# A streaming encoder layer on one core: where background attention runs at the end of two stages, and when the pooling groups are scaled

## The chip, the cores and the metric

The kernel runs on one core of one Trainium2 chip. The metric is the device time of one execution in microseconds (us). A time is the median of several executions, a profile is one execution recorded by the hardware profiler.

## The reference

One layer of a hybrid encoder over 2,080 rows of width 1,024: 2,048 rows of a new stream and 32 rows of a running one, which has 256 cached keys. All in float32.

```python
h = _rmsnorm(x, g_mix)
u = h @ w_in                                   # 1024 -> 512 q, 512 k, 512 v, 512 pooling input
att = _stick_breaking(q, k_all, v_all, ...)    # 8 heads x 64, strictly causal, no softmax:
#   a = sigmoid(z) * prod of sigmoid(-z) over the later keys;  att = a @ v
att = _rmsnorm(att, g_sb_out)
pool = _multiscale_pool(up, ...)               # 4 groups x 128, trailing means over 2/4/8/16 rows minus self,
#   a 128x128 map per group, then _rmsnorm over all four groups with the gain pool_scale
x = x + concat([att, pool]) @ w_out
h2 = _rmsnorm(x, g_ffn)
x = x + (silu(h2 @ w_gate) * (h2 @ w_up)) @ w_down      # D_FF = 2816
gate = sigmoid(_rmsnorm(x, g_ple) @ w_ple_gate)
x = x + (p @ w_ple) * gate
y = _rmsnorm(x, g_final)
```

Keys, values and the last 15 pooling inputs are outputs too.

## The kernel before

**Products.** Activations are kept transposed: features on the 128 partitions, rows along the free axis. Every large product is made exact by splitting both operands into a rounded part and a remainder (`split`: a cast on ScalarE, a subtraction on VectorE, lines 180 and 181), and three matmuls stand for one (`mm3`, lines 215 to 217). Weights go through `wunit`: a 512 KB load on SyncE's queue, a cast on ScalarE (line 199), a subtraction on VectorE (line 200).

**Two chains of stages.** `project` runs three times over pairs of row blocks (`WS`, blocks of 288 or 256 to 384 rows) and makes pooling inputs, values, keys and queries. Then `rest` runs three times over pairs of blocks of 336 or 352 rows (`OS`): output product, feed-forward (gate, up, `down` in groups of four feature tiles), gate of the per-layer embedding (`embed_pair`), final norm. The text calls these three the super-blocks; the third is written in its own way (`tail`).

**Attention as background.** `attention()` is a generator; one `step()` of it issues two score matmuls `z` (line 726; ScalarE turns them into `keep` and `beta`, lines 729 and 730, and so frees the one PSUM bank that `z` has), the scan of `keep` and a product on VectorE (lines 744, 745), the turned weights of an older step (`tp`, line 755, split on ScalarE and VectorE) and the products with the values (`av`, lines 768, 769). `drive` hands out these steps between the pieces of the dense work:

```python
for cost in dense:
    att["credit"] += cost * rate
    while att["gen"] is not None and att["credit"] > 0 and att["next"][0] <= ready:
        att["credit"] -= att["next"][1]
        step()
    if att["credit"] > 0:
        att["credit"] = 0.0
```

`gemm` yields after every two terms (six matmuls) what they cost at 2.4 GHz, `6 * w / 2400.0` for `w` columns: 0.96 for 384, 0.84 for 336, 0.64 for 256. `rate` is 1.1 in the second projection, 1.2 in the third, 0.9 after. A step of a block of three row tiles costs 2 to 3 credits. What is not stepped stays in the generator and comes later; the third super-block starts by stepping all that is left, and the first two step until `NEED` groups are done. The first super-block begins with `yield BUBBLE`, 8 credits at once. Before the change the yields of the last `down` of a super-block count half (`LAST_DOWN`).

TensorE's order is the order in which the program issues its instructions; the other engines' orders come from the framework's planner. Each engine works through its own list in order, and so does each DMA queue.

**Pooling.** `pooled(b, g, ps)` takes the product of group `g` of block `b`, makes the window sums on VectorE and splits the result into a pair of `uu` buffers (three of them). Work that TensorE shall do later is deferred: `defer(n, fn)` runs `fn` after the `n`-th next product (`gemm` ends with `tick()`). `group_map` (the 128x128 map and the squares) runs two products later; after the map of group 3 `pool_norm` makes the sums over the features, `rest` spreads the inverse norm over the partitions (into the single `sq` buffer), and `scaled` multiplies all four groups, splits them and stores them to `HX`, one after another. The products that run meanwhile are those of the values: `v_out` writes `v32` (one of three `u` buffers, which `scaled` takes too), splits it, and sends it out by ScalarE's DMA queue.

Of the kernel before, what the change touches and what calls it, by code (L numbers as in the profile page):

```python
# [12 lines left out]
ALU = mybir.AluOpType  # L13
# [43 lines left out]
PREP_LEAD, PREP_COST = 3, 0.5  # L57
ACT_SLOTS, X_SLOTS = 26, 20
LAST_DOWN = 0.5
RATES = (1.1, 1.2, 0.9, 0.9, 0.9)  # L60


# [17 lines left out]
def stickbreak_step(  # L80
# [8 lines left out]
    V, S, GP, T = nc.vector, nc.scalar, nc.gpsimd, nc.tensor  # L89

    def dma(out, in_, queue=None):
        if out.dtype == F32R:
            out = out.bitcast(F32)
        if in_.dtype == F32R:
            in_ = in_.bitcast(F32)
        (queue or nc.sync).dma_start(out=out, in_=in_)
# [70 lines left out]
    def gcol(key, c):  # L167
        return gt[:, goff[key] + c:goff[key] + c + 1]
# [10 lines left out]
    def split(src, hi, lo):  # L179
        S.copy(hi, src)  # L180
        V.tensor_sub(lo, src, hi.bitcast(F32))  # L181
# [41 lines left out]
    def defer(n, fn):  # L223
        deferred.append([n, fn])
# [126 lines left out]
    def project(sup, pool, st, following):  # L351
# [4 lines left out]
        def tmp(b, tag, bufs=2, dt=F32):  # L356
            return pool.tile([128, WMAX], dt, tag=tag, name=nm(tag), bufs=bufs)[:, :N[b]]

        def pair(b):
            return st["xpool"].tile([128, 2, WMAX], F32R, tag="uu", name=nm("uu"), bufs=3)[:, :, :N[b]]  # L360
# [55 lines left out]
        def pooled(b, g, ps):  # L416

            w = WINS[g]
            up = pool.tile([128, WMAX + 2 * HIST], F32, tag="up", name=nm("up"), bufs=2)[:, :L[b]]
            if b == 0:  # L420
                GP.tensor_copy(up[:, 0:HIST], spT[:, g, :])
                GP.memset(up[:, HIST + DSEQ:HIST + DSEQ + HIST], 0.0)
            else:
                GP.tensor_copy(up[:, 0:HIST], halo[b - 1] [:, g, :])
            for (u0, o0, ln) in segs[b]:
                V.tensor_mul(up[:, u0:u0 + ln], ps[:, o0:o0 + ln], rbc[b][:, o0:o0 + ln])
            GP.tensor_copy(halo[b][:, g, :], up[:, L[b] - HIST:L[b]])
            cur, sh = up, 1
            while sh < w:
                nx = pool.tile([128, WMAX + 2 * HIST], F32, tag="win", name=nm("win"), bufs=2)[:, :L[b]]  # L430
                V.tensor_add(nx[:, 2 * sh - 1:], cur[:, 2 * sh - 1:], cur[:, sh - 1:L[b] - sh])
                cur, sh = nx, 2 * sh
            dd = tmp(b, "u", 3)
            for (u0, o0, ln) in segs[b]:
                V.scalar_tensor_tensor(out=dd[:, o0:o0 + ln], in0=cur[:, u0:u0 + ln], scalar=1.0 / w,
                                       in1=up[:, u0:u0 + ln], op0=ALU.mult, op1=ALU.subtract)
            if b == 0:
                u0 = HIST + DSEQ + HIST
                GP.tensor_mul(dd[:, DSEQ:DSEQ + HIST], cur[:, u0:u0 + HIST], recip[:, g, :])
                GP.tensor_sub(dd[:, DSEQ:DSEQ + HIST], dd[:, DSEQ:DSEQ + HIST], up[:, u0:u0 + HIST])  # L440
            dhl = pair(b)
            dh, dl = dhl[:, 0], dhl[:, 1]
            split(dd, dh, dl)
            if b in hist_of:
                def tail():
                    bank = tp_bank()
                    h0 = hist_of[b][1]
                    T.transpose(bank[:HIST, :128], up[:, h0:h0 + HIST], ident)
                    S.copy(hist[b][:, g * 128:(g + 1) * 128], bank[:HIST, :128])
                    if g == 3:  # L450
                        dma(hist_of[b][0], hist[b])
                defer(1, tail)

            def group_map():
                ps = mm_bank()[:, :N[b]]
                mm3(ps, (wp_hi[:, g, :], wp_lo[:, g, :]), (dh, dl))
                if g == 0:
                    yt[b] = pool.tile([128, 4, WMAX], F32, tag="yt", name=nm("yt"), bufs=2)[:, :, :N[b]]
                S.copy(yt[b][:, g, :], ps)  # L459
                if g == 0:  # L460
                    S.activation(acc[b], yt[b][:, g, :], AF.Square)
                else:
                    sq = tmp(b, "sq", 1)
                    S.activation(sq, yt[b][:, g, :], AF.Square)
                    GP.tensor_add(acc[b], acc[b], sq)
                if g == 3:
                    defer(2, lambda: pool_norm(b))
            defer(2, group_map)

        def pool_norm(b):  # L470
            rp = col_sums([acc[b]], TL[b], SBW)

            def rest():
                rpb = tmp(b, "sq", 1)
                bcast(rp, TL[b], N[b], rpb)


                def scaled():
                    for g in range(4):
                        u = tmp(b, "u", 3)  # L480
                        V.scalar_tensor_tensor(out=u, in0=yt[b][:, g, :], scalar=gcol("pool", g), in1=rpb,
                                               op0=ALU.mult, op1=ALU.mult)
                        uu = pair(b)
                        split(u, uu[:, 0], uu[:, 1])
                        dma(HX[:, 4 + g, :, C0[b]:C0[b] + N[b]].rearrange("a p n -> p a n"), uu)
                defer(1, scaled)
            defer(2, rest)


# [129 lines left out]
        for b in sup:  # L619
            for c in range(2, 4):  # L620
                ps = mm_bank()[:, :N[b]]
                for cost in gemm(ps, proj_terms(ws[c - 2], b)):
                    if b == b1 and nxt and len(nxt["queue"]) > KC:
                        nxt["queue"].popleft()()
                    yield cost
                if b == b0 and nxt:
                    nxt["queue"].popleft()()
                out_qk(b, c, False, ps)
# [247 lines left out]
    def rest(sup, pool, apool):  # L876
# [4 lines left out]
        def tmp(b, tag, bufs=2):  # L881
            return pool.tile([128, OMAX], F32, tag=tag, name=nm(tag), bufs=bufs)[:, :N[b]]
# [190 lines left out]
        def h_terms(w, b):  # L1073
            return [(kpart(w, k), h[b][k]) for k in range(KC)]
# [125 lines left out]
        def down(fs, last):  # L1200
            ng = len(fs)
            oc_n = 8 // ng
            for u in range(KC // oc_n):
                wd = wunit()
                def terms(j, b, f0=0, f1=ng):
                    return [(kpart(wd, i, j * 128, (j + 1) * 128), gvals[fs[i]][b]) for i in range(f0, f1)]

                opened = {}
                if last and tail and u == 0:

                    for j in range(oc_n):
                        for b in sup:
                            ps = opened[j, b] = mm_bank()[:, :N[b]]
                            yield from gemm(ps, terms(j, b, 0, ng // 2), last=False)
                for j in range(oc_n):
                    oc = u * oc_n + j
                    for b in sup:
                        if opened:
                            ps = opened[j, b]
                            yield from gemm(ps, terms(j, b, ng // 2), first=False)  # L1220
                        else:
                            ps = mm_bank()[:, :N[b]]
                            yield from gemm(ps, terms(j, b))
                        V.tensor_add(X[b][oc], X[b][oc], ps)  # L1224
                        if last:
                            ready_h(b, oc, "ple")
# [125 lines left out]
        if not tail:  # L1352
            embed_load(sup[0])

        for cost in down(pend, True):
            yield cost * LAST_DOWN

# [19 lines left out]
        def embed_pair():  # L1379
            for oc in range(KC):  # L1380
                wg, we = wunit(), embed_weight(oc)
                pgs = {}
                for b in sup if oc == 0 else ():

                    pgs[b] = mm_bank()[:, :N[b]]
                    yield from gemm(pgs[b], h_terms(wg, b)[:6], last=False)
                for b in sup:
                    if oc:
                        pgs[b] = mm_bank()[:, :N[b]]
                        yield from gemm(pgs[b], h_terms(wg, b))  # L1390
                    else:
                        yield from gemm(pgs[b], h_terms(wg, b)[6:], first=False)
                    if oc == 0:
                        norm1(b)
                        if b == b1:
                            norm2(b0)
                        embed_in(b)
                        yield 0.8
                for b in sup:
                    yield from gated(b, oc, we, pgs[b])  # L1400
# [153 lines left out]
```

## Time and profile before

| | us |
|---|---|
| median of 3 runs (2855.32 to 2857.84) | 2855.47 |
| the profiled execution, time | 2855.36 |
| its span, first to last instruction | 2853.6 |
| TensorE busy | 2785.0 |
| VectorE busy | 2159.7 |
| ScalarE busy | 1359.5 |

The profiled execution's time is 1.8 us above its span, and 0.1 us from the median. Busy time of TensorE counts a matmul from its start to a modelled end, and successive matmuls overlap, so a busy engine can still run at half clock; the granted clock (PEclk, 1.00 is 2.4 GHz) is read beside it. The projections fill 0 to 557 us, the three super-blocks about 564 to 1,395, 1,395 to 2,205 and 2,205 to the end.

### The profile page before, as it was taken

The numbers are of one execution on the slowest core, as the hardware profiler recorded it, in microseconds if no ns is written. First come the engines' busy times: TensorE is split into PE (matmuls) and PEld (weight loads), VectorE is DVE, ScalarE is ACT, GpSimd is POOL, SyncE is SP. The second block draws the span as 40 slices with busy tenths as digits, with TensorE's granted clock in tenths as the row PEclk, the third lists the DMA queues.
The fourth block names the chain that finished last, engine by engine and source line by source line (L and its number), as shares of the span: only waits on it lengthen the run. The fifth ranks groups of instructions, "written<-read, shape, count | busy, mean of one in ns | idle before, by whom it ended". The sixth has DMA issues, their size and how long they took to land.

```text
span 2853.6 us, 50132 instructions
## 1 busy us (share of the span) xinstructions
PE 2785.0 (98%) x18214; PEld 2740.2 (96%) x18214; DVE 2159.7 (76%) x3681; ACT 1359.5 (48%) x2966; POOL 719.0 (25%) x1222
## 2 busy tenths in 40 slices
PE   8999999899999999999999999999999999999998
PEld 7998889899999999999999999999999999999998
DVE  6476798797878787877888777777764788766677
ACT  5454566564444444455554444444443453333354
POOL 2012233133312222232332212112131343322230
PEclk9999999999999999998999999999999999999999
DMA  6866747783333333323562233333234743222224
GB/s 206 240 197 195 225 153 223 215 243 101 96 116 96 94 96 97 111 86 103 183 195 87 87 108 108 101 105 99 81 100 121 227 125 100 64 78 71 78 82 155
DMA packets 529856, 374.36 MB, mean 131 GB/s; under 512 B 63421, under 2 KB 516861, under 8 KB 529610
## 3 DMA queue, kind: packets, MB, share of 16 engines
q1 hardware_dynamic: 488794, 354.77, 41.6%
q10 hardware_dynamic: 40816, 16.39, 2.1%
q8 instruction: 144, 2.36, 0.4%
q14 instruction: 102, 0.84, 0.1%
HBM read 297.88 MB, written 73.20 MB: 130 GB/s over the span
## 4 chain that ended last, share of the span: by engine, by line
PE 72%; DVE 9%; issue 5%; ACT 3%; DMA 1%; POOL 1%; SPq 0%; ACTq 0%; POOLq 0%; DVEq 0%
PE mm L215 20%; PE mm L216 20%; PE mm L217 19%; PE z L726 4%; PE tp L755 4%; PE av L769 2%; PE av L768 2%; DVE keep L744 2%; DVE wlo L200 1%; DVE wlo L181 1%; DVE beta L745 1%; DVE as L915 1%; DVE aa L181 1%; ACT whi L199 1%; DVE as L181 0%
## 5 line engine op out<-in xcount | busy, mean ns | idle before, releaser
L215 PE MATMUL mm<-as,whi 128*128 128x352 f32 (+1 forms) x3628 | 1202.6, 331 | 5.8 <-DMA as<-hx 3.0
L216 PE MATMUL mm<-as,whi 128*128 128x352 f32 (+1 forms) x3628 | 1166.1, 321 | 0.1
L217 PE MATMUL mm<-as,wlo 128*128 128x352 f32 (+1 forms) x3628 | 1162.0, 320 | 1.2 <-DVE wlo L200 1.1
L215 PEld LDWEIGHTS mm<-as,whi 128*128 128x128 f32 x3628 | 684.2, 189 | 9.5 <-DMA as<-hx 4.0
L217 PEld LDWEIGHTS mm<-as,wlo 128*128 128x128 f32 x3628 | 684.4, 189 | 1.8 <-DVE wlo L200 1.8
L216 PEld LDWEIGHTS mm<-as,whi 128*128 128x128 f32 x3628 | 684.5, 189 | 0.4 <-DVE as L181 0.4
L199 ACT CAST whi<-wraw 128x1024 fp32r<-128x1024 f32 x288 | 302.2, 1049 | 277.2 <-PE mm L216 251.6
L744 DVE TENSOR_TENSOR_SCAN keep<-keep,keep,zeros 128x384 f32<-128x384 f32 (+2 forms) x328 | 320.3, 976 | 106.0 <-ACT keep L729 105.1
L200 DVE TENSOR_TENSOR wlo<-wraw,whi 128x1024 fp32r<-128x1024 f32 x285 | 351.1, 1232 | 57.0 <-ACT whi L199 56.0
L729 ACT ACTIVATE keep<-z 128x384 f32<-128x384 f32 (+3 forms) x464 | 195.5, 421 | 382.6 <-PE z L726 334.3
L741 POOL COPY keep<-keep 128x1 f32<-128x1 f32 (+1 forms) x328 | 147.8, 451 | 485.2 <-DVE keep L744 484.7
L745 DVE TENSOR_TENSOR beta<-beta,keep 128x384 f32<-128x384 f32 (+3 forms) x464 | 235.0, 507 | 32.8 <-POOL beta L734 1.6
L726 PE MATMUL z<-kt,q 128*128 128x384 f32 (+4 forms) x928 | 211.5, 309 | 11.4 <-ACT beta L730 11.3
L181 DVE TENSOR_TENSOR aa<-tp,aa 128x384 fp32r<-128x384 f32 (+4 forms) x472 | 212.8, 451 | 12.7 <-ACT aa L180 11.8
L180 ACT CAST aa<-tp 128x384 fp32r<-128x384 f32 (+4 forms) x472 | 192.8, 408 | 54.4 <-PE tp L755 48.3
L1224 DVE TENSOR_TENSOR xs<-xs,mm 128x352 f32<-128x352 f32 (+1 forms) x288 | 143.6, 509 | 87.6 <-PE mm L217 86.6
L755 PE MATMUL tp<-ident,beta 128*128 128x128 f32 (+1 forms) x1112 | 199.4, 273 | 2.3 <-DVE xt L344 1.5
L215 PE MATMUL mm<-hh,whi 128*128 128x384 f32 (+2 forms) x576 | 198.2, 344 | 2.8 <-ACT yt L459 1.6
L730 ACT ACTIVATE beta<-z 128x384 f32<-128x384 f32 (+3 forms) x464 | 194.4, 419 | 7.0 <-ACT keep L729 5.0
L908 POOL TENSOR_TENSOR acc<-acc,sq 128x352 f32<-128x352 f32 (+1 forms) x111 | 120.6, 1087 | 290.5 <-ACT sq L907 290.5
L216 PE MATMUL mm<-hl,whi 128*128 128x384 f32 (+2 forms) x576 | 185.8, 323 | 1.0 <-DVE hl L338 1.0
L217 PE MATMUL mm<-hh,wlo 128*128 128x384 f32 (+2 forms) x576 | 185.6, 322 | 0.4 <-DVE wlo L200 0.4
(206 smaller groups left out, 4408.5 us busy)
## 6 DMA issues: line engine op xcount, KB each, us to landing
wraw<-in_w_ffn_down_dram SPq DMA_DIRECT2D x66, 512.0 KB, 3.5
wraw<-in_w_ffn_gate_dram SPq DMA_DIRECT2D x58, 512.0 KB, 4.0
wraw<-in_w_ffn_up_dram SPq DMA_DIRECT2D x58, 512.0 KB, 3.9
wraw<-in_w_in_dram SPq DMA_DIRECT2D x48, 512.0 KB, 4.8
wraw<-in_w_out_dram SPq DMA_DIRECT2D x48, 512.0 KB, 5.0
kt<-ks SPq DMA_DIRECT2D x112, 192.0 KB, 2.4
vt<-vs SPq DMA_DIRECT2D x112, 192.0 KB, 2.6
wraw<-in_w_ple_gate_dram SPq DMA_DIRECT2D x32, 512.0 KB, 3.8
```

The lines of the kernel that those rows point to most:

```text
L181: V.tensor_sub(lo, src, hi.bitcast(F32))
L199: S.copy(hi, raw)
L200: eng.tensor_sub(lo, raw, hi.bitcast(F32))
L215: T.matmul(ps, a[0], b[0], start=first, stop=False)
L216: T.matmul(ps, a[0], b[1], start=False, stop=False)
L217: T.matmul(ps, a[1], b[0], start=False, stop=last)
L726: T.matmul(z[:qw, :wi], hd["q"][:, e, qsl], un["k"][:, :wi], start=(e == 0), stop=(e == 1))
L729: S.activation(keep[:qw, :wi], z[:qw, :wi], AF.Sigmoid, scale=-0.125)
L730: S.activation(beta[:qw, :wi], z[:qw, :wi], AF.Sigmoid, scale=0.125)
L744: V.tensor_tensor_scan(rev, rev, zeros[:qw].broadcast_to([qw, wi]), initial=init, op0=ALU.mult, op1=ALU.add)
L745: V.tensor_mul(beta[:qw, :wi], beta[:qw, :wi], keep[:qw, 1:wi + 1])
L755: T.transpose(bank[:kw, qo[i]:qo[i] + qws[i]], un["b"][i][:qws[i], k0:k0 + kw], ident[:qws[i], :qws[i]])
```

## The change

Four edits. (1) The yields of a super-block's last `down` count half up to the twentieth, and nothing from there to the thirty-second, so `drive` issues no step of attention there. (2) The first pieces of `embed_pair` (six terms for each of the two blocks, oc 0) yield 0 instead of their cost. (3) In the third projection the last four query products (c 2 and 3 of both blocks) yield 0.4 of their cost. (4) In the pooling norm the map of group 3 runs one product later, `scaled` treats one group per product instead of four at once, and the first block of a pair gets a buffer of its own (`rpb`) for the spread inverse norm.

```diff
+LAST_QUERIES = 0.4
-            defer(2, group_map)
+            defer(3 if g == 3 else 2, group_map)
         def pool_norm(b):
             rp = col_sums([acc[b]], TL[b], SBW)
             def rest():
-                rpb = tmp(b, "sq", 1)
+                rpb = tmp(b, "rpb" if b == b0 else "sq", 1)
                 bcast(rp, TL[b], N[b], rpb)
-                def scaled():
-                    for g in range(4):
-                        u = tmp(b, "u", 3)
...
-                defer(1, scaled)
+                def scaled(g):
+                    u = tmp(b, "u", 3)
+                    V.scalar_tensor_tensor(out=u, in0=yt[b][:, g, :], scalar=gcol("pool", g), in1=rpb,
+                                           op0=ALU.mult, op1=ALU.mult)
+                    uu = pair(b)
+                    split(u, uu[:, 0], uu[:, 1])
+                    dma(HX[:, 4 + g, :, C0[b]:C0[b] + N[b]].rearrange("a p n -> p a n"), uu)
+                    if g < 3:
+                        defer(1, lambda: scaled(g + 1))
+                defer(1, lambda: scaled(0))
             defer(2, rest)
...
-                    yield cost
+                    yield cost * LAST_QUERIES if last else cost
...
-        for cost in down(pend, True):
-            yield cost * LAST_DOWN
+        for i, cost in enumerate(down(pend, True)):
+            yield cost * LAST_DOWN if i < 20 else 0.0
...
-                    yield from gemm(pgs[b], h_terms(wg, b)[:6], last=False)
+                    for _ in gemm(pgs[b], h_terms(wg, b)[:6], last=False):
+                        yield 0.0
```

## Rows read from the trace of the kernel before

**Rows 1.** The page: engine totals, and the chain that ended last, by engine.

```profile
PE 2785.0 (98%) x18214; PEld 2740.2 (96%) x18214; DVE 2159.7 (76%) x3681; ACT 1359.5 (48%) x2966; POOL 719.0 (25%) x1222
...
PE 72%; DVE 9%; issue 5%; ACT 3%; DMA 1%; POOL 1%; SPq 0%; ACTq 0%; POOLq 0%; DVEq 0%
```

**Rows 2.** What TensorE waited for, whole span: total us, times, longest.

```profile
PE z L726 <- ACT beta L730: 11.3, 11, 3.1
...
PE mm L215 <- DMA as<-hx: 3.0, 3, 1.3
```

**Rows 3.** Stretches: length, busy (count) PE PEld DVE ACT POOL; PEclk, DMA share, GB/s.

```profile
65.00:75.00 10.00, 7.81 (x51) 6.93 (x50) 4.56 (x12) 4.04 (x11) 2.40 (x4) 0.83 0.54 148
...
245.00:260.00 15.00, 13.68 (x100) 13.11 (x99) 10.81 (x26) 8.37 (x25) 0.85 (x4) 0.89 0.90 304
...
555.00:575.00 20.00, 14.56 (x76) 12.42 (x75) 11.93 (x24) 8.25 (x21) 1.58 (x8) 0.83 0.92 312
...
1281.28:1305.88 24.60, 21.46 (x103) 19.19 (x101) 16.36 (x31) 12.35 (x28) 7.54 (x11) 0.67 0.34 100
...
2066.00:2100.00 34.00, 34.00 (x216) 34.00 (x216) 17.92 (x32) 11.02 (x19) 6.19 (x6) 1.00 0.38 117
...
2129.21:2140.74 11.53, 11.09 (x79) 10.67 (x79) 7.52 (x15) 5.94 (x13) 4.93 (x7) 1.00 0.31 91
```

**Rows 4.** TensorE in time, around the end of the first super-block's last down.

```profile
1274.59 0.42 PE L215 MATMUL mm<-as,whi 128*128 128x336 f32 x1 [0.73 <-DVE xs L1224]
...
1275.62 0.51 PE L726 MATMUL z<-kt,q 128*128 128x384 f32 x2
...
1276.57 0.40 PE L215 MATMUL mm<-as,whi 128*128 128x336 f32 x1
...
1287.26 0.31 PE L217 MATMUL mm<-as,wlo 128*128 128x336 f32 x1
...
1290.72 1.01 PE L726 MATMUL z<-kt,q 128*128 128x384 f32 x2 [3.14 <-ACT beta L730]
...
1305.88 0.63 PE L215 MATMUL mm<-as,we 128*128 128x336 f32 x1
```

**Rows 5.** VectorE in time: end of the projections, ends of both last downs.

```profile
561.17 0.41 DVE L181 TENSOR_TENSOR aa<-u,aa 128x256 fp32r<-128x256 f32 x1
...
1266.59 2.71 DVE L915 SCALAR_TENSOR_TENSOR as<-xs,gt,as 128x336 fp32r<-128x336 f32 x1
...
2115.98 2.33 DVE L915 SCALAR_TENSOR_TENSOR as<-xs,gt,as 128x352 fp32r<-128x352 f32 x1 [0.80 <-ACT as L914]
```

**Rows 6.** GpSimd in time, the same moment.

```profile
1266.20 2.73 POOL L200 TENSOR_TENSOR wlo<-wraw,whi 128x1024 fp32r<-128x1024 f32 x1
```

**Rows 7.** TensorE in time: its waits in the three projections.

```profile
67.52 0.58 PE L215 MATMUL mm<-uu,wp_hi 128*128 128x384 f32 x1 [1.82 <-ACT uu L180]
...
95.06 0.39 PE L215 MATMUL mm<-whi,hh 128*128 128x256 f32 x1 [0.88 <-ACT v L546]
...
250.68 0.28 PE L768 MATMUL av<-aa,vt 32*128 32x32 f32 x1 [1.32 <-DVE attT L667]
...
433.48 0.38 PE L215 MATMUL mm<-uu,wp_hi 128*128 128x256 f32 x1 [0.85 <-ACT uu L180]
...
464.46 0.44 PE L726 MATMUL z<-kt,q 128*128 128x128 f32 x2 [1.35 <-ACT beta L730]
```

**Rows 8.** TensorE in time, from the projections to the first output product.

```profile
556.57 0.28 PE L217 MATMUL mm<-hh,wlo 128*128 128x256 f32 x1
...
564.45 0.42 PE L215 MATMUL mm<-as,whi 128*128 128x336 f32 x1 [1.28 <-DMA as<-hx]
```

**Rows 9.** The DMA queue of SyncE in time, the same stretch.

```profile
562.03 10.95 SPq L96 DMA_DIRECT2D as<-hx  x15
```

**Rows 10.** TensorE's score matmuls z: count, ns min/median/max, first and last start.

```profile
L726 PE MATMUL z<-kt,q x928: 178/334/689, 168.5 to 2051.0; 128*128 128x384 f32 x96, 128*128 128x256 f32 x67, 128*128 128x128 f32 x16, 128*32 128x32 f32 x4
```

**Rows 11.** DMA issues of the value stores: count, KB each, median us to landing.

```profile
out_dram<-v ACTq DMA_DIRECT2D x32, 128.0 KB, 3.5
```

More of the change, by code (lines that the diff above doesn't have):

```diff
@@ L473, in rest @@
             def rest():
-                rpb = tmp(b, "sq", 1)
+                rpb = tmp(b, "rpb" if b == b0 else "sq", 1)
                 bcast(rp, TL[b], N[b], rpb)
-                def scaled():
-                    for g in range(4):
-                        u = tmp(b, "u", 3)
[L481 to L485, printed above, removed]
-                defer(1, scaled)
+                def scaled(g):
[8 more added lines that the diff above has]
+                defer(1, lambda: scaled(0))
             defer(2, rest)
```

## The prediction

> **What bounds the kernel now.** I read the engine totals first: TensorE is busy 98% of the span and the chain that ended last runs through it for 72% [rows 1]. So only time in which TensorE stands still, or runs at half clock, can be won; work that is merely moved costs TensorE the same wherever it goes. Then the list of what TensorE waited for: the dearest single kind is `z` waiting for `beta`, 11.3 us in 11 waits [rows 2], that is, attention standing in TensorE's own order before ScalarE and VectorE are through with older work. Then the timeline of TensorE for the places. The longest of these waits, 3.14 us, lies at 1,287 to 1,290 us, just behind the last `down` of the first super-block [rows 4]. Smaller ones lie in the projections [rows 7] and where the output product begins [rows 8]. Last the stretches with their clock: around the long wait the mean granted clock is 0.67, so most of that stretch ran at 1.2 GHz [rows 3].
>
> **Edits 1 and 2, the end of the last down.** The yields cut: 12 of 0.84 at half weight and 6 of 0.84 at full weight, times the rate 0.9, are 4.5 + 4.5 = 9.1 credits, about three steps at up to 3 credits. The trace has three in that place: the `z` at 1,275.62, one in the first piece of `embed_pair`, and the one at 1,290.72 that waits [rows 4]. They are postponed, not saved: one step takes TensorE 0.95 us (1,275.62 to 1,276.57).
>
> What the stall costs is read against the second super-block, where attention is over: its last `z` starts at 2,051.0 [rows 10]. From the first matmul of `embed_pair` to the first of the embedding product the first super-block takes 24.60 us, the second 11.53 us at clock 1.00 for the same products [rows 3]; blocks of 352 instead of 336 columns make the second a little longer, one row piece fewer a little shorter, and I let these cancel. Of the 13.07 us of difference some 2.4 us are three attention steps (one of them short), which remain work. That leaves 10.7 us: the 3.14 us wait, the half clock after it, and smaller waits for the norms. I take off 0.9 us, since a wait like that of 0.73 us for a PSUM bank at 1,274.59 [rows 4] can come once more: VectorE is late before the twentieth yield already. **Gain 9.8 us**; the bounds are 10.7 and 0 (the wait reappears whole at the next product that needs `as` or a norm). In the second super-block the edits find nothing to cut as long as attention ends before its last `down`. All three edits postpone 18 credits, six or seven steps. All attention costs 1,152 credits (8 heads times 8 for the running stream and 3 + 12 + 21 + 30 + 39 + 31 for the blocks) and runs for 1,882 us [rows 10], 0.61 per us, so it ends some 30 us later, at about 2,081. The last `down` there (192 matmuls at 34.00/216 us each [rows 3], 30 us before 2,129.21) starts at about 2,099. The forced steps of the third super-block, which would cost most, are 100 us further off.
>
> **Edit 4, the map of group 3.** TensorE waits 1.82 us for the split of the pooled rows in the first projection and 0.85 us in the third [rows 7]. One value product more in front is 24 x 256 / 2,400 = 2.56 us of matmuls at full clock, more than either wait. Around the first wait the clock of 10 us averages 0.83 [rows 3], which is 1.7 us. Sum 4.4 us; I take **4.0**, with 0 as the lower bound if the value product put in front waits for ScalarE, which is in order behind the same split.
>
> **Edit 4, one group per product.** In the burst four groups of each block stand in VectorE's and ScalarE's lists, and three waits of TensorE lie in these bursts: 0.88, 1.32 and 1.35 us [rows 7]; around the second the clock is 0.89 over 15 us [rows 3], 1.65 us more. Sum 5.2 us. Spread out, the same VectorE work remains and the three `uu` and three `u` buffers stay shared, so I take half, **2.6 us**, bounds 5.2 and a loss (the rival below). The own buffer for block `b0` keeps the spread norm alive over four products without holding up `sq`. It also moves tiles in memory, so some load of the output product can wait for another tile. The nearest row is the 3.0 us that TensorE waits for such loads [rows 2]; as much again is the bound, and I take nothing. `HX` is read much later, and SyncE's queue gets its stores in eight portions over five products instead of eight at once, so the loads of keys and values behind them wait less, not more.
>
> **Edit 3, the last queries.** 8 x 0.96 + 8 x 0.64 = 12.8, times 1.2 = 15.4 credits become 6.1: three to four steps leave the stretch before 556.57. Then VectorE splits the last query at once instead of at 561.17 [rows 5], and SyncE's queue can issue the loads of the output product, 15 of them from 562.03 on [rows 9], one to three us sooner relative to the last projection. But TensorE gets there sooner too, with only the steps of `BUBBLE` to fill the time until the loads land: 7.6 us lie between the last query's matmul and the first output product [rows 8]. TensorE's idle time of 5.4 us in that stretch (20.00 minus 14.56) and its clock of 0.83 [rows 3] therefore mostly stay. **Gain 1.5 us**, bounds 3.4 (the clock's part, 20 x 0.17) and minus 3.0 (the wait for the loads [rows 2] once more).
>
> **Postponed steps.** Six or seven steps land between other products than now, and all later ones shift with them. A `z` waits 11.3 us / 464 steps = 0.02 us on average [rows 2, 10], but one unlucky meeting costs up to 3.14 us and clock. I take **minus 1.0**, bounds plus 2 and minus 6.
>
> **Sum.** 9.8 + 4.0 + 2.6 + 1.5 - 1.0 = 16.9 us off the profiled execution's 2,855.36, which stands 0.1 us from the median: 2,838.5 us. What a measurement of this kernel can tell from no change is 0.2%, 5.7 us.
>
> **A rule against it.** At 1,266.59 VectorE's `as` (line 915) takes 2.71 us, while GpSimd subtracts a gate weight from 1,266.20 on for 2.73 us; in the second super-block it takes 2.33 us, with no attention there [rows 5, 6]. The Trainium skill (SBUF — State Buffer, section Who interferes with whom) says that a VectorE instruction with two SBUF inputs contends with a GpSimd instruction that reads SBUF, and that the second to come is blocked for the whole of the other. This row agrees. By that rule the lateness of VectorE is in part no matter of attention, and this change leaves it in.
>
> **The rivals.**
> First: VectorE's lateness comes from that GpSimd subtraction. All 2.7 us of it then show up as TensorE waiting at the last two terms of the gate, and the clock falls as now, which with the small waits is what remains of 10.7 after 3.14, 7.5 us. Edits 1 and 2 give 10.7 - 2.7 - 7.5 = 0.5 us, the sum is 7.6, the time 2,847.8. For it: the row itself. Against it: the second super-block has the same block and TensorE's clock stays at 1.00 [rows 3]. Chance 0.17.
> Second, the change does not do what it says: the waits only move, to the norm behind the last down and to the next value products, and what is won in one place is lost with the postponed steps. Time 2,853, within 0.2%. For it: VectorE is busy 76% of the span, and 16.36 of the 24.60 us even where TensorE stands [rows 1, 3], so it is a second bound close by. Against it: the longest waits name attention's own results, not those of the products. Chance 0.13.
> Third, slower: one group per product sets `v32` against two `u` of `scaled` in three buffers. Then each value product's `v32` must wait until its predecessor has been sent out, and ScalarE, in order, holds `keep` and `beta` behind it. The 0.88 us for `v` [rows 7] is such a wait. A store takes 3.5 us from issue to landing [rows 11], a value product 2.56 us by its cost: 0.9 us each, doubled where the DMA engines are at 0.90 of their time [rows 3]. Three products in each of three projections at 1.9 us are 17 us, and with edit 4's gains gone (6.6) the time is 2,838.5 + 17 + 6.6 = 2,862. It decides from the point at which the wait exceeds what the PSUM banks in hand cover. Against it: two products' worth of banks are in hand. Chance 0.08.
> The forecast keeps 0.62.
>
> **Numbers.** The forecast's own range is 2,831 (bounds of edits 3 and 4 met: 5 to 8 us more) to 2,846; the first rival lies in 2,843 to 2,852, the second in 2,850 to 2,857. From 2,831 to 2,853 holds eight in ten: above lie the third rival and half of the second, below a few in a hundred. Faster by over 0.2%, below 2,849.8: 0.62 and 0.13 of the first rival, 0.75; within 0.2%: the rest of the first, most of the second and a little of the third, 0.18; slower 0.07.
>
> **What would show it.** Right: no `z` between the twentieth yield and the embedding product, that stretch at 12 to 14 us with clock 1.00, no wait of the map for `uu`, attention ending near 2,081. Wrong: a wait of over 2 us at the last two terms or at the sums of the norm, PEclk 0.5 there; ScalarE waiting for `v` stores in every value product; the first output product still over 7 us behind the last query with longer waits for `as`.

## Result and the profile after

The changed kernel takes 2841.7 us, the median of 6 runs (2838.47 to 2843.89), against 2857.56 for the kernel before beside it (6 runs). The ratio is 0.9944, 95% interval 0.9934 to 0.9955: 16.0 us are won, where 16.9 were forecast. The predicted 2838.5 lies 3.2 us below the measured time, and the time lies inside the range. A second comparison of the same two programs (E12 below) gave 0.9944 again.

The profiled execution took 2842.7 us, its span is 2840.3, so the profiles differ by only 12.7 us. First the engine totals of its page, and the chain that ended last by engine:

```profile
PE 2776.3 (98%) x18214; PEld 2734.5 (96%) x18214; DVE 2152.5 (76%) x3681; ACT 1361.0 (48%) x2966; POOL 711.4 (25%) x1222
...
PE 82%; DVE 8%; issue 3%; ACT 3%; DMA 2%; POOL 1%; ACTq 0%; SPq 0%; POOLq 0%; DVEq 0%
```

The instructions are the same in number as in [rows 1]. What fell is time in which TensorE stood or ran slowly: more of the chain is now TensorE itself. Its waits over the whole span (total us, times, longest):

```profile
PE z L728 <- ACT beta L732: 6.5, 7, 1.8
...
PE mm L216 <- DMA as<-hx: 5.1, 1, 5.1
```

Lines of the changed kernel stand one to three higher than before. The waits of `z` fell from 11.3 to 6.5 us, and the longest of 3.1 us is gone [rows 2]. The loads of the output product went the other way: one wait of 5.1 us stands where three made 3.0.

TensorE in time, first at the entry to the first super-block, from the last query product to the first output product, and then behind that super-block's last `down`, from the first product of the embedding gate to the first embedding product (the number in brackets is the wait before the instruction):

```profile
543.47 0.28 PE L218 MATMUL mm<-hh,wlo 128*128 128x256 f32 x1
543.58 0.52 PE L728 MATMUL z<-kt,q 128*128 128x384 f32 x2
...
545.84 0.62 PE L728 MATMUL z<-kt,q 128*128 128x384 f32 x2 [1.06 <-ACT beta L732]
...
547.48 0.62 PE L728 MATMUL z<-kt,q 128*128 128x384 f32 x2 [0.67 <-ACT beta L732]
...
553.86 0.65 PE L216 MATMUL mm<-as,whi 128*128 128x336 f32 x1 [5.08 <-DMA as<-hx]
...
1265.19 0.40 PE L216 MATMUL mm<-as,whi 128*128 128x336 f32 x1 [0.25 <-DVE xs L1226]
...
1274.19 0.51 PE L728 MATMUL z<-kt,q 128*128 128x256 f32 x2
...
1277.11 1.36 PE L278 MATMUL tp<-ident,r 32*128 32x32 f32 x8 [0.32 <-DVE ss L264]
...
1279.30 0.42 PE L728 MATMUL z<-kt,q 128*128 128x128 f32 x2
...
1280.70 0.63 PE L216 MATMUL mm<-as,we 128*128 128x336 f32 x1
```

And stretches, with the granted clock in the third column from the end (length, busy time and count of each engine, PEclk, DMA share, GB/s):

```profile
60.00:80.00 20.00, 19.75 (x163) 19.00 (x161) 11.40 (x22) 10.97 (x27) 5.98 (x7) 1.00 0.65 173
...
546.00:572.00 26.00, 20.25 (x116) 18.97 (x117) 15.02 (x24) 9.99 (x22) 4.07 (x8) 0.87 0.92 315
...
1265.19:1280.70 15.51, 15.10 (x99) 13.70 (x99) 11.20 (x23) 9.93 (x23) 6.15 (x11) 0.97 0.53 155
1280.70:1285.29 4.59, 4.59 (x26) 4.59 (x25) 3.12 (x8) 1.74 (x6) 0.42 (x3) 0.74 0.69 206
...
2269.40:2282.00 12.60, 12.60 (x63) 12.60 (x64) 5.84 (x15) 5.07 (x13) 0.96 (x2) 0.73 0.48 156
```

From the gate's first product to the embedding product there are 15.51 us with two attention steps in them, where there were 24.60 with three at a clock of 0.67 [rows 3, 4]. The first projection runs at 1.00 past the place of the 1.82 us wait [rows 7]. The entry is worse than before: 10.39 us lie between the last query's matmul and the first output product (553.86 minus 543.47), against 7.88 [rows 8]. The last row is one place that can account for the profiles differing by less than the medians. It follows a wait of 2.14 us in the third super-block. The profiled execution of the kernel before had the same wait there and kept its clock:

```profile
2287.28 0.75 PE L256 MATMUL tp<-ones,acc 128*128 128x1 f32 x6 [2.12 <-DVE acc L908]
...
2287.28:2300.00 12.72, 12.72 (x83) 12.72 (x84) 8.72 (x21) 6.58 (x16) 0.96 (x2) 1.00 0.59 198
```

12.60 us at 0.73 are 3.4 us; with them the profiles would differ by 16.1 us, as the medians do. None of the four edits touches that place.

### The profile page after: what moved, and what is told of

It reads as the page before. It is cut to its first block, busy times and chain, and to the rows that moved or that the text cites. A ratio compares the mean times of both kernels' runs of the same rounds, so it can differ in the third digit from the quotient of the medians.

```text
span 2840.3 us, 50159 instructions
## 1 busy us (share of the span) xinstructions
PE 2776.3 (98%) x18214; PEld 2734.5 (96%) x18214; DVE 2152.5 (76%) x3681; ACT 1361.0 (48%) x2966; POOL 711.4 (25%) x1222
## 4 chain that ended last, share of the span: by engine, by line
PE 82%; DVE 8%; issue 3%; ACT 3%; DMA 2%; POOL 1%; ACTq 0%; SPq 0%; POOLq 0%; DVEq 0%
PE mm L216 23%; PE mm L217 22%; PE mm L218 22%; PE z L728 4%; PE tp L757 4%; PE av L770 2%; PE av L771 2%; DVE wlo L201 1%; DVE keep L746 1%; ACT whi L200 1%; DVE win L432 1%; DVE beta L747 1%; PE tp L278 1%; PE tp L257 1%; DVE as L917 0%
```

## The experiments

Theory: edits 1 and 2 take away a meeting of attention with a late VectorE (the wait of `z` and the half clock behind it), the later map takes away the waits for `uu`, the spread smooths VectorE's work, and edit 3 brings little, because the loads set the entry. Rivals: VectorE is late because of GpSimd's subtraction beside it; the waits only move; the spread costs waits for buffers. In all, 12 kernels ran, each beside the kernel before on its chip (its medians 2857.9, 2856.15 and 2856.47 in the three jobs). Gains in us are one minus the ratio, times that median.

**E1, edits 1 and 2 alone.**

```diff
-        for cost in down(pend, True):
-            yield cost * LAST_DOWN
+        for i, cost in enumerate(down(pend, True)):
+            yield cost * LAST_DOWN if i < 20 else 0.0
...
-                    yield from gemm(pgs[b], h_terms(wg, b)[:6], last=False)
+                    for _ in gemm(pgs[b], h_terms(wg, b)[:6], last=False):
+                        yield 0.0
```

> Edits 1 and 2 alone (no attention in the last 12 yields of the last down, none in the first pieces of the gate). Theory: the stall behind the last down was attention waiting for attention, and it goes. The stretch from the first gate product to the first embedding product falls from 24.6 us to 13 to 16 us, its clock rises from 0.67 to above 0.9, and the whole kernel gains 8 to 10 us (ratio about 0.9967). Rival (VectorE is late because of GpSimd's subtraction, or the wait moves to the norm): a wait of 2 us or more in the same place, gain under 2 us.

Measured: 2845.44 us, ratio 0.9957 [0.9943, 0.9972], 12.3 us won (8.0 to 16.3). TensorE in time, and the stretch from the gate to the embedding product:

```profile
1273.43 0.42 PE L215 MATMUL mm<-as,whi 128*128 128x336 f32 x1 [0.74 <-DVE xs L1224]
...
1279.89 0.39 PE L215 MATMUL mm<-as,whi 128*128 128x336 f32 x1 [0.63 <-DVE xs L1224]
...
1292.69 0.59 PE L726 MATMUL z<-kt,q 128*128 128x384 f32 x2
...
1279.89:1293.72 13.83, 13.74 (x91) 12.47 (x92) 9.55 (x20) 8.41 (x18) 6.39 (x9) 1.00 0.38 115
```

The only `z` of the stretch comes 1.03 us before the embedding product, the clock is 1.00, and 13.83 us stand in place of 24.60. Two waits for VectorE's sums of the `down` (`xs`, which frees a PSUM bank), 0.74 and 0.63 us, stay. The mean granted clock of every run is on record too: on average 0.9909 in the 23 runs of the kernel before and 0.9948 in E1's six. The 0.0039 between them are 11 us of the span, an estimate that takes TensorE as the pace all along: nearly all that E1 won is TensorE's clock.

**E6, edit 1 alone** (the first half of the diff above).

> Edit 1 alone: no credit from the twentieth yield of a super-block's last down on, embed_pair's first pieces yielding their cost as before. Edits 1 and 2 together took 12.5 us. Theory that the credit is the cause, wherever it is handed out: 4.5 of 9.1 credits are cut, the step in the first piece of embed_pair and the waiting z behind it stay, gain 3 to 5 us, ratio 0.998 to 0.999, and the z after the down still waits over 1 us for beta. Theory that VectorE's lateness at the end of the down is built up by the steps inside the down: with these gone the z in embed_pair finds its bank free, no wait over 1 us there, gain 9 us or more, ratio 0.997 or less.

Measured: 2853.16 us, ratio 0.9991 [0.9982, 0.9999], 2.6 us won (0.3 to 5.1). TensorE in time, and the stretch from the gate to the embedding product:

```profile
1284.75 0.51 PE L726 MATMUL z<-kt,q 128*128 128x384 f32 x2
...
1291.58 1.54 PE L1093 MATMUL tp<-ident,pn 32*128 32x32 f32 x8 [1.99 <-DVE aa L181]
...
1280.97:1300.12 19.15, 17.16 (x96) 15.68 (x96) 12.68 (x24) 10.33 (x22) 6.86 (x11) 0.83 0.32 97
```

The step inside `embed_pair` no longer waits, as the second theory had it, but it does not win the 9 us that theory named. Its work stands on VectorE ahead of the norm's, and TensorE's next turn (`pn`, the rows of the per-layer input) waits 1.99 us for the last of it, the split `aa`. VectorE in time:

```profile
1288.65 1.01 DVE L744 TENSOR_TENSOR_SCAN keep<-keep,keep,zeros 128x384 f32<-128x384 f32 x1
1289.79 0.56 DVE L745 TENSOR_TENSOR beta<-beta,keep 128x384 f32<-128x384 f32 x1
...
1290.96 0.56 DVE L181 TENSOR_TENSOR aa<-tp,aa 128x384 fp32r<-128x384 f32 x1
1291.44 0.27 DVE L263 TENSOR_SCALAR ss<-tp 32x1 f32<-32x1 f32 x3
```

The clock falls behind this wait too, though for a shorter time: the stretch takes 19.15 us at 0.83, where it was 24.60 at 0.67 and, with both edits, 13.83 at 1.00.

**E7, edit 2 alone** (the second half of the diff).

> Edit 2 alone: embed_pair's first pieces hand out no credit, the yields of the last down all count half as before. Edits 1 and 2 together stood at 0.9957, edit 1 alone at 0.9991 (its profile had no wait of z at the end of the down, but a wait of 1.99 us of the final norm's turn for VectorE's split, and the half clock as before). Theory that one step is one too many wherever it stands, and that both edits are needed: TensorE still waits over 1 us between the down and the embedding product and the clock falls there, ratio 0.998 to 1.000. Rival, that the step inside embed_pair is what does the harm: no wait over 1 us and clock 1.00 there, ratio 0.995 to 0.997, all of what the two edits win.

Measured: 2856.81 us, ratio 0.9999 [0.9991, 1.0008]: nothing. TensorE in time, and the same stretch:

```profile
1276.40 0.51 PE L726 MATMUL z<-kt,q 128*128 128x384 f32 x2
...
1292.60 0.77 PE L1093 MATMUL tp<-ident,pn 32*128 32x32 f32 x4 [1.27 <-DVE ss L263]
...
1282.06:1300.34 18.28, 16.63 (x91) 14.66 (x89) 13.08 (x24) 10.09 (x22) 6.42 (x10) 0.82 0.33 99
```

Here the late steps of the `down` are the ones left, and now the same turn waits for the norm's sums (`ss`, line 263) and the clock falls. This profile's stretch is 6.3 us shorter than that of the kernel before, and yet the medians show nothing won; where E7 loses it again stays open. 2.6 and 0.3 us alone, 12.3 together: in both profiles the steps that remain leave a wait of over 1 us with a fallen clock behind it.

**E8, the changed kernel without GpSimd's subtraction.** The first column of the gate's weights is split by VectorE.

```diff
-            plan_col(w_pgate, (i % KC) * 128, V if i else GP)
+            plan_col(w_pgate, (i % KC) * 128, V)
```

> The changed kernel with the first column of the embedding gate's weights split by VectorE instead of GpSimd, so that no GpSimd subtraction stands beside VectorE's product for the second block at the end of the last down. Forecast: that blocked 2.3 us instruction holds up nothing in the changed kernel (TensorE did not wait for it), so the time stays at 0.994 to 0.995 of the kernel before, and VectorE's product takes under 1 us. First rival (the GpSimd subtraction is what makes VectorE late): another 2 to 5 us are won, ratio 0.9925 to 0.9937, with the stretch from the last down to the embedding product down from 15.5 us. Third possibility: the subtraction itself, now 1 to 2 us of VectorE's own time, makes the norm late, ratio above 0.9955.

Measured: 2841.01 us, ratio 0.9952 [0.9939, 0.9965], the changed kernel's time within the intervals. VectorE (DVE) and GpSimd (POOL) in time, first in the changed kernel, then in this one:

```profile
1251.55 2.39 POOL L201 TENSOR_TENSOR wlo<-wraw,whi 128x1024 fp32r<-128x1024 f32 x1
1251.98 2.33 DVE L917 SCALAR_TENSOR_TENSOR as<-xs,gt,as 128x336 fp32r<-128x336 f32 x1 [0.81 <-ACT as L916]
```

```profile
1250.25 1.24 DVE L201 TENSOR_TENSOR wlo<-wraw,whi 128x1024 fp32r<-128x1024 f32 x1 [0.33 <-ACT whi L200]
1251.14 1.11 POOL L910 TENSOR_TENSOR acc<-acc,sq 128x336 f32<-128x336 f32 x1 [0.73 <-ACT sq L909]
1251.41 1.22 DVE L917 SCALAR_TENSOR_TENSOR as<-xs,gt,as 128x336 fp32r<-128x336 f32 x1
```

The blocked product of 2.33 us becomes 1.22, not under 1 us as expected: GpSimd's sum of squares now runs beside it, and products of this form that begin while GpSimd is idle take 0.57 us in both profiles. VectorE does the subtraction itself in 1.24, and the time stays: the 0.9925 to 0.9937 that the first rival asked for lies outside the interval. VectorE's lateness from this subtraction is real and decides nothing here.

**E3, edit 4 whole, E4, the later map alone, and E5, the spread alone.**

```diff
-            defer(2, group_map)
+            defer(3 if g == 3 else 2, group_map)
```

E4 is this line; E5 is the rest of edit 4 (`rpb`, and `scaled` for one group at a time); E3 is both.

> Edit 4 alone (map of group 3 one product later, one group per product, own buffer). Theory: 6 to 9 us gained, nearly all of it in the first projection and some in the third (ratio about 0.9975). Rival: the spread groups make ScalarE wait for the value stores at every product and half of the gain is lost, 3 us or less.

> Only the later map of group 3; the four groups still in one burst, no buffer of its own. Theory: the waits of 1.82 us and 0.85 us for the split go, and with the clock 4 us are gained (0.9986); the wait of 0.88 us for the value evacuation stays. Rival: the wait only moves to the value product put in front, gain under 1 us.

> Edit 4 without the later map: one group per product and the own buffer rpb, group 3's map after two products as before. Forecast as it was predicted: the bursts are gone, 2.6 us less than the kernel before, ratio about 0.999. Rival, suggested by the later map alone at 0.9978 against 0.9969 for all of edit 4: the spread moves the same work and gains under 1 us; the first z then starts near 168.5 us as before, and the wait of the map for uu in the first projection stays at about 1.8 us, ratio 0.999 to 1.001. Third rival of the prediction: value products wait for buffers, ratio above 1.002 and ScalarE waiting for stores of v.

Measured: E3 2849.16 us, ratio 0.9969 [0.9957, 0.998], 8.9 us won; E4 2851.23, 0.9978 [0.9967, 0.9989], 6.3 us (3.1 to 9.4); E5 2852.18, 0.9988 [0.9979, 0.9996], 3.4 us (1.1 to 6.0). What the matmuls of the map waited for, in E5, over the span (us, times):

```profile
  ACT uu L180: 2.7, 2
  DVE uu L181: 0.5, 1
```

In all eight profiles with the later map this list is empty. The first `z` of attention tells what the first projection gained. In the six profiles without the later map it starts between 166.3 and 168.5 us, in the eight with it between 161.9 and 164.0 (161.9 and 164.0 are one program, the changed kernel, twice); the means, 167.3 and 163.1, are 4.1 us apart. The spread takes away TensorE's wait of 0.88 us for `v` in the first projection [rows 7] and brings it none for a buffer; what VectorE waits for is told with the third rival below.

**E9, the changed kernel without the spread.**

```diff
-                rpb = tmp(b, "rpb" if b == b0 else "sq", 1)
+                rpb = tmp(b, "sq", 1)
...
-                def scaled(g):
...
-                    if g < 3:
-                        defer(1, lambda: scaled(g + 1))
-                defer(1, lambda: scaled(0))
+                def scaled():
+                    for g in range(4):
...
+                defer(1, scaled)
```

> All of the change but the spread: edits 1 to 3 and group 3's map one product later, the four groups scaled in one burst, one buffer for the spread inverse norm. If the spread is worth what was predicted (2.6 us), this kernel stands at 0.9953 of the one before, 0.0009 above the changed kernel's 0.9944. If the spread is worth nothing, it stands at 0.994 to 0.995, and the last turn of the first projection, the first z (near 162 us) and the last z come out as in the changed kernel within 2 us. If the burst is the better form, it is below 0.993.

Measured: 2842.93 us, ratio 0.9953 [0.9941, 0.9965]. E9 against the changed kernel, E4 against E3 and E5 by itself put the spread at 0.0009, 0.0009 and 0.0012, about 2.5 to 3.4 us; only E5's interval leaves out a gain of zero.

**E2, edit 3 alone.**

```diff
+LAST_QUERIES = 0.4
...
-                    yield cost
+                    yield cost * LAST_QUERIES if last else cost
```

> Edit 3 alone (the last four query products hand out 0.4 of their credits). Theory: the output product starts some 10 us earlier less the three to four postponed steps, so 1 to 2 us are gained, and one long wait for the loads of 4 to 5 us takes the place of several short ones (ratio 0.9993 to 1.0). Rival: VectorE is freed for the whole start of the first super-block too, gain 4 us or more (0.9985). Second rival: nothing is gained since TensorE has less to do until the loads land, or up to 3 us are lost.

Measured: 2852.62 us, ratio 0.9982 [0.9973, 0.9991], 5.1 us won (2.6 to 7.7). TensorE in time:

```profile
555.48 0.28 PE L218 MATMUL mm<-hh,wlo 128*128 128x256 f32 x1
...
565.28 0.65 PE L216 MATMUL mm<-as,whi 128*128 128x336 f32 x1 [4.50 <-DMA as<-hx]
...
1286.97 1.01 PE L727 MATMUL z<-kt,q 128*128 128x384 f32 x2 [4.28 <-ACT beta L731]
```

The last query is earlier (555.48 against 556.57) and the first output product later (565.28 against 564.45 [rows 8]). The postponed steps come back behind the last `down`, where `z` now waits 4.28 us. By the same measure the 5.1 us of the medians are TensorE's clock: it averages 0.9939 in E2's twelve runs, against 0.9909 before, which by the estimate of E1 is 8.6 us, more than was won. In this profile one such place is the stretch from the gate to the embedding product, 1278.34 to 1302.15 us, with a clock of 0.86 in spite of the longer wait. Why the clock holds better there is not shown.

**E11, edits 1 and 2 with the later map alone** (neither edit 3 nor the spread).

> Edits 1 and 2 with the later map, and neither edit 3 nor the spread. If the parts add up, 0.9957 and 0.9978 give 0.9935, and with edit 3 left out the first output product starts near 576 us as with the later map alone. If the whole wins less than its parts because edits 3 and 1 spend the same room (postponed steps come back elsewhere), this kernel is as fast as the changed one, 0.994 to 0.995. If edit 3 is worth its 0.0018 in company too, it stands at 0.9955 to 0.9965.

Measured: 2838.26 us, ratio 0.9938 [0.9926, 0.995], 17.7 us won. E1 and E4 add up to 0.9935, so these parts add. TensorE's waits from 540 to 582 us:

```profile
PE mm L215 <- DMA as<-hx: 2.7, 3, 1.4
PE z L726 <- ACT beta L730: 1.6, 2, 1.2
PE av L769 <- DVE aa L181: 0.8, 2, 0.6
```

5.1 us of waits, close to the 5.4 of the kernel before, and not the single long one of the changed kernel. E9 is this kernel plus edit 3, and stands 0.0015 above it, where edit 3 alone stood 0.0018 below the kernel before. The two intervals of E9 and E11 overlap, so it isn't shown that edit 3 costs time in company; that it is not worth its 5.1 us there is (minus 4.3, give or take 4.9, from the intervals' half widths of 3.4 us each). The mean clock of the runs says the same, 0.9948 in E9 and 0.9964 in E11: 4.5 us.

**E10, the changed kernel with more attention at the entry.**

```diff
-BUBBLE = 8.0
+BUBBLE = 16.0
```

> The changed kernel with BUBBLE at 16 credits instead of 8, so two to four more steps of attention stand between the last query and the first output product, where TensorE of the changed kernel waits 5.08 us in one piece for as<-hx. Theory that the loads set that moment and that the steps fit into the time: the first output product starts at the same distance from the last query's product, the wait is under 2 us, and 2 to 4 us are won against the changed kernel, ratio 0.9930 to 0.9937. Rival, that attention is itself bound there by VectorE's scans: TensorE waits for beta instead of for as, the first output product comes as late or later, ratio 0.994 to 0.996.

Measured: 2837.97 us, ratio 0.993 [0.9917, 0.9942], 20.0 us won, the lowest of all. TensorE in time, and a stretch of 26 us, to be held against that of the changed kernel above:

```profile
546.11 0.28 PE L218 MATMUL mm<-hh,wlo 128*128 128x256 f32 x1
546.22 0.52 PE L728 MATMUL z<-kt,q 128*128 128x384 f32 x2
...
555.20 0.48 PE L728 MATMUL z<-kt,q 128*128 128x256 f32 x2
...
557.01 0.63 PE L216 MATMUL mm<-as,whi 128*128 128x336 f32 x1
...
549.00:575.00 26.00, 23.24 (x138) 21.31 (x137) 20.28 (x37) 13.44 (x32) 7.74 (x17) 0.93 0.95 320
```

The first output product follows the last query by 10.90 us, hardly later than the 10.39 of the changed kernel. Six steps of attention lie in that time instead of three, the wait for `as` is gone, `z` waits 2.9 us there instead of 1.7, and the clock of the stretch is 0.93 instead of 0.87. The first load has landed at 555.9 us, so the steps run 1.1 us past the moment that the loads set.

**E12, the changed kernel again**, on the chip of E7, E10 and E11.

> The changed kernel itself, on the same chip as the three others: the measure for what they win or lose against it. By the first comparison 0.9944 [0.9934, 0.9955]. The sum of the parts measured alone (0.9957, 0.9982, 0.9969) is 0.9908. If the parts add up, it comes out at or below 0.993; if the whole is less than its parts, at 0.994 to 0.9955.

Measured: 2841.61 us, ratio 0.9944 [0.9932, 0.9956]. E10 is 3.6 us below it by the medians and E11 3.4; their intervals overlap with its own, so that either beats the changed kernel is likely and not settled.

## Why the prediction came out

**The forecast's way and its sum hold; the terms in it are off and cancel.** The edits alone win 12.3 (edits 1 and 2), 8.9 (edit 4) and 5.1 us (edit 3), 26.3 together, where 17.9 were forecast; the whole wins 16.0. The gains were put 8.4 us too low, and what the edits take from one another 9.3 us too low. That the sum came within 0.9 us is therefore luck, while the main stall and its price were read rightly.

**Edits 1 and 2**, forecast 9.8, bounds 0 and 10.7: 12.3, interval 8.0 to 16.3. The reading against the second super-block named the right stretch and about its price: 13.83 us at 1.00 in E1, where 12 to 14 were said. The price was read from one profile, and the clock does not fall each time. E5 keeps the three steps and a wait of 3.15 us, and loses far less behind it than the kernel before:

```profile
1280.62:1300.55 19.93, 16.70 (x102) 14.98 (x101) 15.97 (x30) 11.96 (x27) 6.88 (x11) 0.91 0.32 92
```

The same stretch takes 24.02 us at 0.71 in E3 and 24.60 at 0.67 in E4. So how much of the price one execution pays varies, and it is the mean clock of E1's runs that carries the reading. In the changed kernel itself two steps come between the turns of the norm, the stretch takes 15.51, and a wait of 0.32 us is followed by a clock of 0.74 for 4.6 us; behind the same wait in E9 the clock is 1.00. The statement that no `z` stands between the twentieth yield and the embedding product was wrong: only the yields of `embed_pair`'s first six terms count nothing, and credit flows again from the terms and norms behind them. What the prediction did not see is that neither edit is worth much without the other (E6, E7).

**The first rival** (GpSimd's subtraction) falls with E1 and E8. E1 keeps the block whole and wins 12.3 us all the same:

```profile
1265.43 2.70 DVE L915 SCALAR_TENSOR_TENSOR as<-xs,gt,as 128x336 fp32r<-128x336 f32 x1
```

In E8 the block is shortened and the time is the same. The Trainium skill (SBUF — State Buffer, Who interferes with whom) describes that block, one engine held for the whole of the other's instruction. The rows agree: the product ends 0.37 us behind GpSimd's instruction in the changed kernel and 0.38 us in E8, 2.33 and 1.22 us after it began. That it sets the end of the `down` they don't show.

**The second rival** (the waits only move) is true of E6 and E7 and of the entry, and not of the whole. **The third** (spread and value stores share buffers) has its mechanism and not its price. VectorE's scaled product (`u`) in the changed kernel waits for stores of `v` (total us, times, longest):

```profile
DVE u L480 <- DMA out_dram<-v: 8.3, 5, 3.0
```

In the kernel before that was 2.5 us in two waits. It is the pooling product that waits, not the value product, ScalarE's wait for such a store is 1.1 us in all, and TensorE does not stand still for it: E5 is faster, not slower.

**The later map**, forecast 4.0: 6.3 us by the ratio of E4, 4.1 by the first `z`. The waits for `uu` are gone in all eight profiles with it. **The spread**, forecast 2.6: 2.5 to 3.4, at the edge of what the runs can tell.

**Edit 3** is the step that failed. The prediction had SyncE's queue issue the loads of the output product one to three us sooner relative to the last projection, saw that TensorE would reach the entry sooner too, and still took 1.5 us won. What it put down as the sign of being wrong, the first output product over 7 us behind the last query with longer waits for `as`, is what the profile shows: 10.39 us (7.88 in the kernel before) and 5.08 us. Counted from the last query product the first load goes out no sooner, 3.58 us behind it (547.05) against 3.43 (560.00), and it takes longer (KB, us from issue to landing, first in the kernel before, then in the changed kernel):

```profile
as<-hx SPq DMA_DIRECT2D x1, 336.0 KB, 4.4
```

```profile
as<-hx SPq DMA_DIRECT2D x1, 336.0 KB, 6.8
```

In all eight profiles without edit 3 the first load takes 4.3 to 4.7 us and the output product starts 7.8 to 8.2 us behind the last query; in all six with it these are 5.9 to 6.8 and 9.5 to 10.9 us. What does go out sooner is the load behind the first, 0.56 us after it (547.61) where it was 2.03 (562.03 [rows 9]). That loads issued so close slow one another, at 0.92 of the DMA engines' time, is likely and was not tested. E10 shows what the time is good for: three more steps in it cost 0.5 us.

**Postponed steps**, forecast minus 1.0, bounds plus 2 and minus 6: the parts and the whole are 10.3 us apart, give or take 6.6 by their intervals, and no other term of the sum stands for that. E11 tells where: edits 1, 2 and the map add up, and the sum breaks when edit 3 joins (E9: 13.4 us won, where 17.7 and 5.1 would make 22.8). The rows show the longer wait at the entry. Alone, edit 3 made up for it by a better clock (E2); why it does not in company stays open.

**The end of attention** was put near 2,081. The score matmuls and the turns `pn` of the per-layer input's rows in the changed kernel (ns min/median/max, first and last start):

```profile
L728 PE MATMUL z<-kt,q x928: 178/334/460, 161.9 to 2055.0; 128*128 128x384 f32 x96, 128*128 128x256 f32 x67, 128*128 128x128 f32 x16, 128*32 128x32 f32 x4
...
L1095 PE MATMUL tp<-ident,pn x38: 234/273/331, 1272.7 to 2233.0; 128*128 128x128 f32 x24, 96*128 96x96 f32 x8, 32*128 32x32 f32 x2, 48*128 48x48 f32 x2
```

The last `z` comes 4.0 us later than in [rows 10], while the last turn `pn` comes 17.9 us sooner than the 2250.9 it had. So against the dense work attention ends 21.9 us later. The 30 us were too many, and the time won had not been taken off. The conclusion, that attention ends before the second super-block's last `down`, holds.

## What to carry over

When background work meets a stage whose helper engines are late, the steps that remain decide: half of the cut leaves a shorter wait in another place, and the clock falls behind that one. Work taken away in front of a point that a transfer sets does not bring that point nearer; look for what TensorE would do until the loads land before thinning it out. Gains of edits measured alone add up for some pairs and not for others: test them in company, and try the whole without each part. Where the gain is TensorE's clock, read its mean over many runs beside the one profile.

## What the runs showed of the hardware

TensorE's clock does not fall in the same way behind the same wait each time. The wait of 2.10 to 2.14 us in the third super-block, which no edit touches, is in all fourteen profiles. Over the 12.6 us behind it the granted clock is 1.00 in one of them (the kernel before), 0.86 in seven and 0.73 in six. The changed kernel, profiled twice, has 0.73 once and 0.86 once (E12). Its first six runs spread over 5.4 us, as much as its smaller edits are worth. A difference of a few us between two profiles is therefore read only together with the granted clock of each stretch.

The first of a row of loads takes longer where the others follow it closely: 336 KB landed 4.3 to 4.7 us after issue where the second load came 2.03 us later, and 5.9 to 6.8 us where it came 0.56 to 0.84 us later. The fourteen profiles show the two side by side; no run tests the spacing by itself.
